# Six instead of four of every sixteen tiles turned on VectorE, with the moves placed elsewhere and the loads divided differently, in an RMSNorm and matmul kernel

## The chip, the cores and the metric

One core of a Trainium2 chip. The metric is the device time of one execution in microseconds; a time in the text is the median of a kernel's runs. The span in a profile, from the first to the last instruction of one profiled execution, is some 2 us shorter (208.1 us in an execution of 210.44 us). Ratios are computed as the mean time of one kernel's fast runs over that of the other's of the same rounds, so they are not quite the ratio of the medians that are quoted.

## The reference

```python
# x: 16 x 1024 x 512 fp32, gamma: 512, weight: 512 x 768, eps 1e-5
rms = np.sqrt(np.mean(x ** 2, axis=-1, keepdims=True) + eps)
x_norm = x / rms * gamma
return np.matmul(x_norm, weight)       # 16 x 1024 x 768 fp32
```

The kernel treats x as 128 tiles of 128 rows. It reads 33.6 MB of x and writes 50.3 MB of results.

## The kernel before

GpSimd casts x to bf16, two bf16 values are treated as one fp32 word, and the tile is turned so that features lie on the partitions. TensorE multiplies the turned tile by the weights (which hold gamma already), and ScalarE (even tiles) or VectorE (odd tiles) scales the product by 1/rms on its way out of PSUM, where the program has TensorE put its products. Three accumulators in PSUM go round. Two tiles make a pair, numbered j; eight pairs make a group of sixteen tiles, which is also the unit of loading.

Twelve tiles of a group (in the first group all sixteen) are turned by TensorE, by transposes put between the matmuls of the pair two earlier, and copied out of PSUM by VectorE. The other four are turned by VectorE alone, in 16 "moves", each of which transposes 32 x 32 blocks (in the page 32 x 256 fp32, 435 ns each).

```python
x_first, x_size = stretches(XG, {0: [2, 2, 4, 8], **{g: [8, 8] for g in (1, 4, 5, 6, 7)}})
# a group that is not named here is one load of 16 tiles, 4 MB
...
def cast_quad(q):                                  # four tiles to be turned on VectorE
    quads[q] = quad_in.tile([P, 4, D], BF16, name="xq")
    nc.gpsimd.tensor_copy(out=quads[q], in_=held(x_tiles, XG, 4 * q, 4))
    ...                                            # puts 16 moves in quad_moves
def move_quad(n):
    for _ in range(min(n, len(quad_moves))):
        dst, src = quad_moves.pop(0)
        nc.vector.transpose(out=dst, in_=src)
...
for j in range(1, NP):
    load_until(...)                                # SyncE issues loads and stores, in this order
    ...                                            # casts of later tiles, GpSimd
    if (2 * j + 2) % XG == 0 and 2 * j + 2 < NT:
        cast_quad((2 * j + 2 + XG - 4) // 4)
    elif 2 * j >= XG:
        move_quad(3)                               # VectorE: moves first ...
    for pair in norm_turns.get(j, []):
        norms_of_group(pair)                       # ScalarE: squares of pair j + 4, from the fp32 load
    ...
    for i, engine in ((2 * j, nc.scalar), (2 * j + 1, nc.vector)):
        a = accumulator()                          # three go round
        matmuls(i, a, range(K), feed)              # feed: transposes of pair j + 2, then VectorE's copy
        finish_tile(i, a, engine)                  # ... then the copy, then the scaling
```

The order on each engine is set by this program. VectorE's scaling stands behind the moves of its pair (in the trace three moves start at 157.97 us, the copy at 159.35, the scaling at 160.08), and ScalarE's scaling behind the squares of a tile four pairs ahead (a square that waited 4.32 us for its load starts at 50.20 us, the scaling behind it at 51.44).

## Time and profile before

| | before |
|---|---|
| time, 3 runs | 210.66 us (210.31 to 210.72) |
| span of the profiled run | 208.1 us |
| TensorE, VectorE, ScalarE busy | 94%, 72%, 69% |
| bytes moved, mean rate | 85.65 MB, 412 GB/s |

The first fence is the page's summary of the chain of work that ended last; the second is from the view of waits, with total us, number and longest.

```profile
PE 71%; DMA 21%; SPq 2%; ACT 1%; POOL 1%; DVE 0%; issue 0%; ACTq 0%; POOLq 0%
```

```profile
POOL xb L94 <- DMA xt<-in_x_dram: 113.0, 16, 18.0
...
PE ops L198 <- ACT ot L178: 2.0, 1, 2.0
```

Once it is running, TensorE waits for another engine for 2.0 us in one place.

### The profile page before, as it was taken

Reading aid. Unit: us, or ns where it says so; the run is one execution under the profiler, and the core shown is the slowest. Engines: PE = TensorE matmul, PEld = TensorE weight load, DVE = VectorE, ACT = ScalarE, POOL = GpSimd, SP = SyncE. Lnnn points to the kernel's source line nnn. Section 1 sums busy time; section 2 is a strip of 40 time slices with the busy share of each in tenths; the row PEclk is TensorE's granted clock in tenths of the full one; section 3 lists DMA queues with packets and bytes.
Section 4 is the critical chain, followed back from the end, with each engine's and each line's share of the span. In section 5 each row is a group of like instructions: output and inputs, shape, how many; then the busy total and the mean of one; then the engine's idle time right before and its main releaser. Section 6 shows DMA issues by size and latency. Waiting matters only on the chain.

```text
span 208.1 us, 3335 instructions
## 1 busy us (share of the span) xinstructions
PE 195.1 (94%) x1238; PEld 129.9 (62%) x1238; DVE 149.6 (72%) x255; ACT 144.5 (69%) x343; POOL 59.9 (29%) x34
## 2 busy tenths in 40 slices
PE   7899999996999999999999999999999999999930
PEld 2466776663666666676667666776667666776610
DVE  0456647997379984999579984999579984999520
ACT  4698897753977877677867877677867877673310
POOL 3237652003900390065200670007500373000000
PEclk9999999999999999999999999999999999999996
DMA  6999999999999999999999999999999999994996
GB/s 252 419 438 441 331 396 435 459 449 390 437 439 438 405 439 409 408 403 431 428 411 436 441 430 430 420 431 439 430 438 408 424 444 435 424 439 203 453 413 267
DMA packets 5490, 85.65 MB, mean 412 GB/s; under 512 B 610, under 2 KB 612, under 8 KB 1380
## 3 DMA queue, kind: packets, MB, share of 16 engines
q1 hardware_dynamic: 5472, 85.46, 97.4%
q8 instruction: 9, 0.15, 0.3%
q14 instruction: 5, 0.04, 0.0%
q10 hardware_dynamic: 4, 0.00, 0.0%
HBM read 35.13 MB, written 50.33 MB: 411 GB/s over the span
## 4 chain that ended last, share of the span: by engine, by line
PE 71%; DMA 21%; SPq 2%; ACT 1%; POOL 1%; DVE 0%; issue 0%; ACTq 0%; POOLq 0%
PE ops L198 63%; DMA xt<-in_x_dram 21%; PE tp L135 8%; SPq L83 1%; POOL xb L94 1%; DVE ot L180 0%; ACT jk L98 0%; SPq L236 0%; ACT ot L178 0%; POOLq L94 0%; ACTq L178 0%; ACTq L98 0%
## 5 line engine op out<-in xcount | busy, mean ns | idle before, releaser
L198 PE MATMUL ops<-w_bf,xT 128*128 128x512 bf16 (+1 forms) x800 | 147.7, 326 | 2.6 <-ACT ot L178 2.0
L198 PEld LDWEIGHTS <-xT 128*128 128x128 bf16 x800 | 78.3, 98 | 48.4 <-issue 3.0
L178 ACT ACTIVATE ot<-ops,rstd 128x768 f32<-128x768 f32 x64 | 57.6, 899 | 45.3 <-PE ops L198 44.6
L98 ACT ACTIVATE jk<-xt 128x512 bf16<-128x512 f32 x128 | 78.8, 619 | 6.2 <-DMA xt<-in_x_dram 6.2
L94 POOL CAST xb<-xt 128x2048 bf16<-128x2048 f32 (+3 forms) x21 | 46.3, 2218 | 113.0 <-DMA xt<-in_x_dram 113.0
L180 DVE TENSOR_SCALAR ot<-ops,rstd 128x768 f32<-128x768 f32 x64 | 64.8, 1013 | 12.5 <-PE ops L198 12.0
L135 PE MATMUL tp<-ident_f,xb 128*128 128x128 f32 x200 | 54.2, 276 | 0.8 <-POOL xb L94 0.7
L142 DVE COPY xT<-tp 128x1024 bf16<-128x1024 bf16 (+1 forms) x53 | 34.5, 654 | 24.8 <-PE tp L135 24.1
L174 DVE STREAM_TRANSPOSE xTq<-xq 32x256 f32<-32x256 f32 x112 | 48.7, 435 | 1.9
L198 PE MATMUL ops<-w_bf,xTq 128*128 128x512 bf16 x224 | 42.8, 326 | 0.0
L135 PEld LDWEIGHTS tp<-ident_f,xb 128*128 128x128 f32 x200 | 28.5, 143 | 4.9 <-POOL xb L94 2.5
L198 PEld LDWEIGHTS <-xTq 128*128 128x128 bf16 x224 | 22.0, 98 | 12.3
L98 ACT ACTIVATION_READ_ACCUMULATOR jk<-xt 128x1 f32 x128 | 24.4, 191 | 0.0
L160 POOL CAST xq<-xt 128x2048 bf16<-128x2048 f32 x7 | 13.3, 1894 | 0.0
L104 DVE RECIPROCAL rstd<-rms 128x8 f32<-128x8 f32 (+3 forms) x20 | 3.9, 193 | 7.7 <-ACT rms L102 7.5
L102 ACT ACTIVATE rms<-ssq,eps_sb 128x8 f32<-128x8 f32 (+3 forms) x20 | 6.0, 299 | 0.6
L254 PE MATMUL ops<-warm 128*128 128x512 bf16 x12 | 5.2, 587 | 1.2 <-DVE eps_sb L247 1.2
L254 PEld LDWEIGHTS <-warm 128*128 128x128 bf16 x12 | 1.4, 128 | 2.9 <-issue 1.7
L178 ACT ACTIVATE w_bf<-w_f,g_sb 128x768 bf16<-128x768 f32 x2 | 1.9, 935 | 1.4 <-DMA w_f<-in_weight_dram 1.1
L267 DVE COPY g_sb<-tp 128x4 f32<-128x4 f32 x1 | 0.2, 161 | 3.2 <-PE tp L265 3.2
L231 ACT ACT_TABLE_LOAD x1 | 1.3, 1283 | 1.3 <-PEq L338 1.3
L180 DVE TENSOR_SCALAR w_bf<-w_f,g_sb 128x512 bf16<-128x512 f32 (+2 forms) x3 | 1.4, 481 | 0.1
(10 smaller groups left out, 1.9 us busy)
## 6 DMA issues: line engine op xcount, KB each, us to landing
out_dram<-ot SPq DMA_DIRECT2D x13, 3072.0 KB, 15.8
xt<-in_x_dram SPq DMA_DIRECT2D x11, 2048.0 KB, 18.5
xt<-in_x_dram SPq DMA_DIRECT2D x2, 4096.0 KB, 20.2
out_dram<-ot SPq DMA_DIRECT2D x5, 1536.0 KB, 9.9
w_f<-in_weight_dram SPq DMA_DIRECT2D x2, 768.0 KB, 5.6
out_dram<-ot SPq DMA_DIRECT2D x2, 768.0 KB, 16.5
xt<-in_x_dram SPq DMA_DIRECT2D x2, 512.0 KB, 5.3
xt<-in_x_dram SPq DMA_DIRECT2D x1, 1024.0 KB, 9.2
```

What stands on the lines that cost most here:

```text
L94: engine.tensor_copy(out=xb_tiles[i // 8][:, i % 8:i % 8 + n, :], in_=held(x_tiles, XG, i, n))
L98: nc.scalar.activation(out=jk, in_=held(x_tiles, XG, i)[:, 0, :], func=AF.Square, accum_out=ssq)
L102: nc.scalar.activation(out=rms[:, :n], in_=ssq[:, :n], func=AF.Sqrt, scale=1.0 / D, bias=eps_sb)
L104: nc.vector.reciprocal(out=rstd[:, :n], in_=rms[:, :n])
L135: nc.tensor.transpose(out=tp_tiles[j][:, t, h, :], in_=words[:, lo:lo + P], identity=ident_f)
L142: nc.vector.tensor_copy(out=dst[:, t:t + n, :], in_=src[:, t:t + n, :])
L160: nc.gpsimd.tensor_copy(out=quads[q], in_=held(x_tiles, XG, 4 * q, 4))
L174: nc.vector.transpose(out=dst, in_=src)
L178: nc.scalar.mul(out=dst, in_=src, mul=r)
L180: nc.vector.tensor_single_scalar(out=dst, in_=src, scalar=r, op=mybir.AluOpType.mult)
L198: nc.tensor.matmul(out=acc[:, lo:hi], lhsT=xT_tiles[i // 2][:, i % 2, k // 2, :, k % 2], rhs=w_bf[:, k, lo:hi], start=(k == 0), stop=(k == ...
L254: nc.tensor.matmul(out=spare[:, :WIDE], lhsT=warm[:, :P], rhs=warm, start=True, stop=True)
```

## The change

Its intent: take two more tiles of each group off TensorE, whose transposes cost it time (by the trace about 0.11 us each); put the moves into the pairs in which TensorE still has transposes, since those last longer (3.04 us against 2.60); and bring tiles 32 to 47 in two loads so that the first half lands earlier.

```diff
-    x_first, x_size = stretches(XG, {0: [2, 2, 4, 8], **{g: [8, 8] for g in (1, 4, 5, 6, 7)}})
+    x_first, x_size = stretches(XG, {0: [2, 2, 4, 8], **{g: [8, 8] for g in (1, 2, 4, 5, 6)}})
 ...
-    B = 32
-    quads, quad_moves = {}, []
+    B, TURNED = 32, 6
+    quad_moves = []
 ...   (cast_to_turn casts six tiles instead of four; still 16 moves, each of half as many elements again)
-            elif j % 8 == 6 and j + 2 < NP:
-                cast(2 * j + 12, nc.gpsimd, 4)
-            if (2 * j + 2) % XG == 0 and 2 * j + 2 < NT:
-                cast_quad((2 * j + 2 + XG - 4) // 4)
-            elif 2 * j >= XG:
-                move_quad(3)
+            elif j % 8 == 5 and j + 3 < NP:
+                cast_to_turn(j // 8 + 1)
+                cast(2 * j + 14, nc.gpsimd, 2)
+            if j > 6:
+                move_quad({3: 4, 4: 0, 5: 0}.get(j % 8, 3))
 ...
-            elif j + 2 < NP and quad_of(j + 2) is None:
+            elif j + 2 < NP and not turned_on_vector(j + 2):
```

The list of groups in eights gains group 2 and loses group 7 (tiles 112 to 127).

More of the change, by code (lines that the diff above doesn't have):

```diff
@@ L148, in transpose_tile, with turned_on_vector, cast_to_turn @@
         evac(i // 2, i % 2, 1)
-    B = 32
-    quads, quad_moves = {}, []
-    def quad_of(j):
-        return j // 2 if (2 * j) % XG >= XG - 4 and 2 * j >= XG else None
-    def cast_quad(q):
-        quads[q] = quad_in.tile([P, 4, D], BF16, name="xq")
-        nc.gpsimd.tensor_copy(out=quads[q], in_=held(x_tiles, XG, 4 * q, 4))
-        turned = quad_out.tile([P, 4, 2, P, 2], BF16, name="xTq")
-        for n in range(2):
-            xT_tiles[2 * q + n] = turned[:, 2 * n:2 * n + 2]
-        words = quads.pop(q).rearrange("p t d -> p (t d)").bitcast(F32).rearrange("p (a w) -> p a w", w=P)
+    B, TURNED = 32, 6
+    quad_moves = []
+    def turned_on_vector(j):
+        return (2 * j) % XG >= XG - TURNED and 2 * j >= XG
+    def cast_to_turn(group):
+        first = (group + 1) * XG - TURNED
+        straight = quad_in.tile([P, TURNED, D], BF16, name="xq")
+        nc.gpsimd.tensor_copy(out=straight, in_=held(x_tiles, XG, first, TURNED))
+        turned = quad_out.tile([P, TURNED, 2, P, 2], BF16, name="xTq")
+        for n in range(TURNED // 2):
+            xT_tiles[first // 2 + n] = turned[:, 2 * n:2 * n + 2]
+        words = straight.rearrange("p t d -> p (t d)").bitcast(F32).rearrange("p (a w) -> p a w", w=P)
         out_words = turned.rearrange("p t h m c -> p (t h m c)").bitcast(F32).rearrange("p (a m) -> p a m", m=P)
```

## The prediction

> **What bounds the kernel now.** I read the page first, then the chain of waits in order of time, then VectorE's and GpSimd's timelines. From the page, the engines' totals, the DMA row and the four groups that the change touches:
> ```profile
> PE 195.1 (94%) x1238; PEld 129.9 (62%) x1238; DVE 149.6 (72%) x255; ACT 144.5 (69%) x343; POOL 59.9 (29%) x34
> ...
> DMA  6999999999999999999999999999999999994996
> ...
> L180 DVE TENSOR_SCALAR ot<-ops,rstd 128x768 f32<-128x768 f32 x64 | 64.8, 1013 | 12.5 <-PE ops L198 12.0
> L135 PE MATMUL tp<-ident_f,xb 128*128 128x128 f32 x200 | 54.2, 276 | 0.8 <-POOL xb L94 0.7
> L142 DVE COPY xT<-tp 128x1024 bf16<-128x1024 bf16 (+1 forms) x53 | 34.5, 654 | 24.8 <-PE tp L135 24.1
> L174 DVE STREAM_TRANSPOSE xTq<-xq 32x256 f32<-32x256 f32 x112 | 48.7, 435 | 1.9
> ```
> TensorE is busy 94%, VectorE has slack on average, and the DMA engines are full until nearly the end. The chain of waits, in order of time:
> ```profile
> 29.96 20.16 DMA xt<-in_x_dram
> 50.12 0.02 issue
> ...
> 51.53 0.80 ACT ot L178
> 52.33 0.04 issue
> 52.37 1.68 PE ops L198 x9
> ```
> Up to 50 us the path is the 4 MB load of tiles 32 to 47 landing; from 52.37 on it is TensorE without a gap. In the chain's later rows eight matmuls without transposes take 1.30 us a tile; four matmuls take 0.65 us and four with a transpose 0.76, so a transpose costs TensorE about 0.11 us, not its 276 ns. A group of 16 tiles repeats every 23.42 us: 16 x 1.30 + 24 x 0.11. Below I count in pairs of tiles: 2.60 us without transposes, 3.04 with.
>
> The stall at 50 us teaches what a late load does. ScalarE squares tile 32 at the start of pair 12, before it scales that pair's first output; while it waits, TensorE runs three tiles (three accumulators) and stops 2.0 us at the fourth. From landing (50.12) to TensorE's restart (52.37) are 2.25 us.
>
> VectorE, in the pairs that now carry moves:
> ```profile
> 157.97 1.33 DVE L174 STREAM_TRANSPOSE xTq<-xq 32x256 f32<-32x256 f32 x3
> 159.35 0.69 DVE L142 COPY xT<-tp 128x1024 bf16<-128x1024 bf16 x1
> 160.08 1.02 DVE L180 TENSOR_SCALAR ot<-ops,rstd 128x768 f32<-128x768 f32 x1
> 161.13 1.33 DVE L174 STREAM_TRANSPOSE xTq<-xq 32x256 f32<-32x256 f32 x3
> ```
> The same place comes round after 3.16 us here (9.37 us for three pairs to 167.34, so 3.12 on average) against TensorE's 3.04: VectorE is already full here and falls back 0.1 us a pair. And GpSimd at the last group:
> ```profile
> 164.82 3.60 POOL L94 CAST xb<-xt 128x4096 bf16<-128x4096 f32 x1 [16.21 <-DMA xt<-in_x_dram]
> 169.71 1.89 POOL L94 CAST xb<-xt 128x2048 bf16<-128x2048 f32 x1 [1.29 <-DMA xt<-in_x_dram]
> 171.55 1.89 POOL L160 CAST xq<-xt 128x2048 bf16<-128x2048 f32 x1
> ```
> Each cast begins as its load lands. The first halves land at 115.6, 139.9 and 164.7 us, some 24.5 us apart: the queue is slower than TensorE's 23.42, which eats its lead. The last first half lands at 164.7, just in time for ScalarE at pair 52 (about 165.7).
>
> [...] the trace holds about 427 GB/s from 95 to 189 us, so I take the queue as full: a load's landing is set by the bytes queued before it, not by when TensorE is ready.
>
> **The change part by part.**
> (1) TensorE loses 28 transposes (seven groups, one more pair each): 28 x 0.11 = 3.1 us, 0.43 a group.
> (2) Tiles 32 to 47 arrive in two loads. The first half, queued where it was, lands about 4.9 us sooner (2.1 MB at 427 GB/s), near 45.2, before ScalarE asks at 45.9. The 2.0 us stall goes.
> (3) The list of groups loaded in eights also loses the last one: tiles 112 to 127 now come in one 4 MB load. It is whole only when the old second half was, about 169.6 us. ScalarE restarts TensorE 2.25 us later, at 171.85, with tile 107, which before began near 169.55. After that tile pair 54 begins at 173.15, not 170.86: 2.3 us late, whatever was won earlier. GpSimd agrees: cast of eight tiles 169.7 to 173.3, needed at the start of pair 54.
> (4) Each of the 112 moves has 384 elements for 256: [...]. VectorE's full pair becomes 3.12 + 3 x 0.133 = 3.52 us against 3.04. Before, moves stood in four pairs with transposes and two without; now in five with and one without, so less is made good in between.
> The consequence: an odd tile's accumulator must be scaled before the tile three later starts. Before, moves begin 1.30 us after their pair starts. If they begin at s, the first pair's scaling ends at s + 3.53 (1.73 moves, 0.05, 0.73 copy, 1.02), the fifth's 4 x 3.52 later, at s + 17.61. The pair that needs that accumulator would start 5 x 3.04 + 2.60 = 17.8 us after the first. With s = 1.30 TensorE is held about 1.15 us per group: more than the 0.43 saved. The period becomes about 24.2 us: five steady groups (2 to 6) give back 3.7 us, more than the roughly 1.2 us still in hand at pair 14 (2.0 + 0.43 less a hold of 1.2 in the first group). So by DVE alone pair 54 starts near 173.4, about where the late load puts it.
> (5) Moves now begin two pairs earlier (pair 54, not 56), and their six-tile cast runs behind the eight-tile one. In the last group it ends at 173.3 + 2.75 = 176.0 (2.75: between 1.89 for four tiles and 3.60 for eight). VectorE, in order, waits for it until 176.0 with the copies and scalings behind it. From there 17.61 + 0.05 puts pair 60 at 193.7; before it started at 189.1. Pairs 60 to 63 and the last stores are unchanged.
> Sum: +2.3 (late load) - 0.43 (last group's transposes) + 2.7 (VectorE held to 176.0, then too slow) = +4.6 us. 210.66 + 4.6 = 215.2 us.
>
> **Rivals.**
> A, the intent: the moves hide and TensorE's 3.1 us and the stall's 2.0 come off: 205.6 us. For it: TensorE is 94% busy, VectorE 72%. Against it: the landing at 169.6 and VectorE's 3.12 in just those pairs.
> B, only the load counts: VectorE's lag stays within the accumulators' slack, and its wait in the last group is absorbed: +2.3 - 0.43, some 212.5 us. For it: no VectorE lag stops TensorE now, and a lag of 0.3 us at pair 52 had 1.2 to spare. Against it: the fifth full pair and the cast's end.
> C, moves grow in full proportion, 0.65 us: VectorE's pair is 3.77 us, over 1 us more is lost in every group, VectorE alone sets the pace, and the total is near 219 us. [...]
> D, TensorE's earlier stores slow the loads: little in it, since loads and stores share one queue in program order and it is already full.
>
> **Range and chances.** The late load leaves little room under 212.5. Above that the size hangs on VectorE's pair: 3.35 instead of 3.52 gives 0.7 us less, C several more, and the landing may shift by 0.5 us. The 2% line lies at 214.9, just below my estimate. I predict 215.2 us, 8 times in 10 between 212.9 and 218.0; faster by over 2% 0.04, within 2% 0.41, slower by over 2% 0.55.
>
> **What would show it right or wrong.** The stall at 50 us should be gone, with ScalarE's wait for tile 32 under 0.5 us. The moves should average about 570 ns. TensorE's period in groups 2 to 6 should be near 24.2 us with gaps released by VectorE's scaling; 23.0 would mean that the lag is absorbed (B). ScalarE should wait for the last load, and GpSimd's eight-tile cast begin near 169.7; a start near 165 would refute step 3. VectorE should show idle time ahead of the moves that GpSimd's cast ends, at the last group above all. If the span is below 205, A holds and my reading of the queue is wrong; if the moves take 650 ns, C.

That a move grows by 0.133 us, on which step 4 rests, was not shown by the kernel before: its 112 moves all have one size. The changed kernel's page shows it, 569 ns for 384 elements against 435 for 256, 0.134 us more.

## The result, and the profile after

The changed kernel takes 214.53 us (213.98 to 214.84, 6 runs) against 210.94 us for the kernel before (210.31 to 211.93, 6 runs): ratio 1.0165, 95% interval 1.0137 to 1.0193. Its profiled span is 212.6 us, 4.5 us more.

The lines of the page that answer to those in the prediction:

```profile
PE 193.7 (91%) x1187; PEld 126.1 (59%) x1210; DVE 159.4 (75%) x248; ACT 144.3 (68%) x343; POOL 59.9 (28%) x34
...
DMA  6999999999999999999999999999999999591897
...
DVE 49%; DMA 18%; PE 14%; issue 7%; POOLq 3%; ACT 3%; POOL 2%; SPq 1%; DVEq 0%
...
L181 DVE TENSOR_SCALAR ot<-ops,rstd 128x768 f32<-128x768 f32 x64 | 64.8, 1014 | 24.0 <-PE ops L199 23.1
...
L175 DVE STREAM_TRANSPOSE xTq<-xq 32x384 f32<-32x384 f32 x112 | 63.8, 569 | 5.2 <-POOL xq L161 3.2
...
L135 PE MATMUL tp<-ident_f,xb 128*128 128x128 f32 x172 | 46.7, 277 | 0.6 <-POOL xb L94 0.3
```

VectorE's busy share rose only from 72% to 75%, yet the chain that ended last runs over VectorE for 49% of the span, where it ran over TensorE for 71% before. A share averaged over the span does not show in which pairs an engine is full. The moves take 569 ns, and 28 transposes are gone.

VectorE in the pairs with moves, from its timeline (start, us, what); it answers to the second VectorE fence of the prediction:

```profile
112.83 1.74 DVE L175 STREAM_TRANSPOSE xTq<-xq 32x384 f32<-32x384 f32 x3
114.59 0.69 DVE L142 COPY xT<-tp 128x1024 bf16<-128x1024 bf16 x1
115.32 1.02 DVE L181 TENSOR_SCALAR ot<-ops,rstd 128x768 f32<-128x768 f32 x1
116.37 1.74 DVE L175 STREAM_TRANSPOSE xTq<-xq 32x384 f32<-32x384 f32 x3
```

Here the place comes round after 3.54 us; over the five pairs from 102.43 to 119.85 us the mean is 3.48. TensorE needs 3.04 for such a pair. After the fifth it has to stop, as its timeline shows in brackets (idle time, and what ended it):

```profile
116.04 3.20 PE L199 MATMUL ops<-w_bf,xT 128*128 128x256 bf16 x19
119.87 2.76 PE L199 MATMUL ops<-w_bf,xT 128*128 128x512 bf16 x15 [0.63 <-DVE ot L181]
```

The nineteen matmuls are the last three of pair 34 and the sixteen of pair 35. The next tile, 72, needs the accumulator of tile 69, which VectorE has just scaled. The last group looks different. GpSimd's timeline and then VectorE's:

```profile
170.15 3.60 POOL L94 CAST xb<-xt 128x4096 bf16<-128x4096 f32 x1 [20.63 <-DMA xt<-in_x_dram]
173.70 2.75 POOL L161 CAST xq<-xt 128x3072 bf16<-128x3072 f32 x1
```

```profile
173.76 1.02 DVE L181 TENSOR_SCALAR ot<-ops,rstd 128x768 f32<-128x768 f32 x1 [2.52 <-PE ops L199]
176.48 1.73 DVE L175 STREAM_TRANSPOSE xTq<-xq 32x384 f32<-32x384 f32 x3 [1.70 <-POOL xq L161]
```

The 4 MB load lands at 170.0 us, GpSimd casts eight tiles, then the six, and VectorE's moves start at 176.48, the moment this ends (176.45). Finally the waits:

```profile
ACT jk L98 <- DMA xt<-in_x_dram: 7.1, 4, 3.2
PE ops L199 <- DVE ot L181: 6.6, 14, 0.7
...
PE ops L199 <- ACT ot L179: 0.8, 1, 0.8
```

Fourteen waits of TensorE for VectorE are new. Some records of matmuls are missing (1187 of 1210), so part of the waits may go unlisted; I therefore take distances between VectorE's scalings of odd tiles, one of each group, for the account:

| stage (pair of the odd tile scaled) | before, us | changed, us | difference |
|---|---|---|---|
| pair 13 reached at | 53.87 | 52.36 | -1.51 |
| 13 to 21 | 23.51 | 23.77 | +0.26 |
| 21 to 29 (moves of tiles 58 to 63) | 23.42 | 25.36 | +1.94 |
| 29 to 37 and 37 to 45, each | 23.42 | 23.78 | +0.36 |
| 45 to 53 (last load awaited) | 23.42 | 24.71 | +1.29 |
| 53 to 61 (last group) | 23.42 | 25.57 | +2.15 |
| pair 61 reached at | 194.48 | 199.33 | +4.85 |

So the changed kernel is ahead after the stall at 50 us, gives back 0.4 us in an undisturbed group, and loses most in three places that have to do with a load that is whole.

### The profile page after: what moved, and what is told of

The parts are those of the page before. It is cut to its first block, busy times and chain, and to the rows that moved or that the text cites.

```text
span 212.6 us, 3246 instructions
## 1 busy us (share of the span) xinstructions
PE 193.7 (91%) x1187; PEld 126.1 (59%) x1210; DVE 159.4 (75%) x248; ACT 144.3 (68%) x343; POOL 59.9 (28%) x34
## 4 chain that ended last, share of the span: by engine, by line
DVE 49%; DMA 18%; PE 14%; issue 7%; POOLq 3%; ACT 3%; POOL 2%; SPq 1%; DVEq 0%
DVE xTq L175 24%; DMA xt<-in_x_dram 18%; DVE ot L181 17%; PE ops L199 13%; DVE xT L142 7%; POOLq L352 3%; ACT jk L98 2%; POOL xq L161 1%; DVE rstd L104 1%; POOL xb L94 1%; SPq L83 1%; PE tp L135 1%; SPq L237 0%; ACT ot L179 0%; SPq L196 0%
## 5 line engine op out<-in xcount | busy, mean ns | idle before, releaser
L199 PE MATMUL ops<-w_bf,xT 128*128 128x512 bf16 (+1 forms) x673 | 127.4, 324 | 7.1 <-DVE ot L181 6.0
L199 PEld LDWEIGHTS <-xT 128*128 128x128 bf16 x688 | 67.3, 98 | 46.4 <-issue 7.1
L94 POOL CAST xb<-xt 128x1024 bf16<-128x1024 f32 (+3 forms) x21 | 40.4, 1934 | 108.3 <-DMA xt<-in_x_dram 89.5
L175 DVE STREAM_TRANSPOSE xTq<-xq 32x384 f32<-32x384 f32 x112 | 63.8, 569 | 5.2 <-POOL xq L161 3.2
L199 PE MATMUL ops<-w_bf,xTq 128*128 128x256 bf16 (+1 forms) x328 | 60.8, 324 | 1.8 <-ACT ot L179 0.8
L135 PE MATMUL tp<-ident_f,xb 128*128 128x128 f32 x172 | 46.7, 277 | 0.6 <-POOL xb L94 0.3
L199 PEld LDWEIGHTS <-xTq 128*128 128x128 bf16 x336 | 32.9, 98 | 21.3 <-issue 1.8
L142 DVE COPY xT<-tp 128x1024 bf16<-128x1024 bf16 (+1 forms) x46 | 29.1, 633 | 6.9 <-PE tp L135 6.4
L135 PEld LDWEIGHTS tp<-ident_f,xb 128*128 128x128 f32 x172 | 24.5, 143 | 6.5 <-POOL xb L94 2.3
L161 POOL CAST xq<-xt 128x3072 bf16<-128x3072 f32 x7 | 19.2, 2747 | 8.7 <-DMA xt<-in_x_dram 5.8
```

The source lines that it names most:

```text
L94: engine.tensor_copy(out=xb_tiles[i // 8][:, i % 8:i % 8 + n, :], in_=held(x_tiles, XG, i, n))
L135: nc.tensor.transpose(out=tp_tiles[j][:, t, h, :], in_=words[:, lo:lo + P], identity=ident_f)
L142: nc.vector.tensor_copy(out=dst[:, t:t + n, :], in_=src[:, t:t + n, :])
L161: nc.gpsimd.tensor_copy(out=straight, in_=held(x_tiles, XG, first, TURNED))
L199: nc.tensor.matmul(out=acc[:, lo:hi], lhsT=xT_tiles[i // 2][:, i % 2, k // 2, :, k % 2], rhs=w_bf[:, k, lo:hi], start=(k == 0), stop=(k == ...
```

## The experiments

Two theories of the slowdown were open besides the intended gain: the whole last load, and VectorE's overfull pairs. With the two kernels, the first four runs cross three lists of loads (that of the kernel before, that of the changed one, and both groups in eights) with the two ways of turning. The kernel before took 210.77 us in the rounds of these four (7 runs).

**1. The kernel before, group 2 in eights.**

```diff
-g in (1, 4, 5, 6, 7)
+g in (1, 2, 4, 5, 6, 7)
```

> The kernel before with one change: tiles 32 to 47 in two loads of eight (the last group stays in eights). Theory (the queue is full and in order, VectorE does not hold TensorE): the 2.0 us stall at 50 us goes and nothing takes its place, because the last first half still lands near 164.7 us and ScalarE then asks at about 163.0 us, which three tiles of accumulators cover. Expect 208.6 us (ratio 0.990), no wait of TensorE for ScalarE at 50 us. Rival (the stall is only moved: TensorE runs into the loads later): 210.5 us, with a new TensorE wait near 165 us.

Measured: 210.47 us (209.86 to 210.90), ratio 0.997 (0.9924 to 1.0016). The theory's time is a miss, though its mechanism is there: the stall is gone, TensorE waits for nobody at 165 us, and VectorE starts the last scaling at 197.56 us instead of 199.68. The rival's new wait near 165 us is not there either. The 2.1 us are lost after the last scaling. The view of windows shows it. Its columns are the stretch and its length in us, the busy time of TensorE, its weight loads, VectorE, ScalarE and GpSimd (with the number of instructions), the granted clock, the share of the 16 DMA engines' time, and GB/s. First the kernel before, then this one:

```profile
188.00:189.00 1.00, 1.00 (x9) 0.66 (x7) 0.94 (x4) 0.66 (x1) 0.00 (x0) 1.00 0.63 270
189.00:190.00 1.00, 1.00 (x8) 0.61 (x7) 0.97 (x2) 0.00 (x0) 0.00 (x0) 1.00 0.29 123
190.00:191.00 1.00, 1.00 (x8) 0.61 (x7) 0.97 (x2) 0.42 (x1) 0.00 (x0) 1.00 0.12 49
```

```profile
188.00:189.00 1.00, 1.00 (x8) 0.61 (x7) 0.97 (x2) 0.54 (x1) 0.00 (x0) 1.00 0.35 147
189.00:190.00 1.00, 1.00 (x8) 0.60 (x7) 0.96 (x3) 0.36 (x1) 0.00 (x0) 1.00 0.98 418
...
204.00:205.00 1.00, 0.00 (x0) 0.00 (x0) 0.00 (x0) 0.00 (x0) 0.00 (x0) 0.50 0.27 111
205.00:206.00 1.00, 0.00 (x0) 0.00 (x0) 0.00 (x0) 0.00 (x0) 0.00 (x0) 0.50 0.12 49
206.00:207.00 1.00, 0.00 (x0) 0.00 (x0) 0.00 (x0) 0.00 (x0) 0.00 (x0) 0.50 0.03 12
```

Before, the engines are partly idle from 188 to 191 us (shares 0.63, 0.29 and 0.12), as the store of tiles 112 to 119 is issued only at 190.80 us. Here that store comes 2.1 us sooner, at 188.68; at the end the share falls to 0.27, 0.12 and 0.03, but something is moved until 207. In the kernel before the same stretches from 204 to 206 us still move 430 and 479 GB/s. The last store lands at 207.34 us, against 207.21 before. So the DMA transfers, not TensorE, end last, and they end at 49 and 12 GB/s. By the shares, 0.12 would be two of the 16 engines and 0.03 half of one; that a few engines lag is an estimate of mine from these shares, since the trace does not tell packets by engine. The two runs 8 and 9 test whether the transfers set the end.

**2. The kernel before, with the changed kernel's list of loads.**

```diff
-g in (1, 4, 5, 6, 7)
+g in (1, 2, 4, 5, 6)
```

> The kernel before with the changed kernel's whole list of loads: tiles 32 to 47 in eights, tiles 112 to 127 in one 4 MB load; four tiles turned as before. Theory (the whole last load costs by itself): ScalarE waits for it until about 169.7 us and TensorE stops some 4 us near 168 us, so 2.3 us more than before: 212.9 us (ratio 1.011). Rival (the whole load is hidden by VectorE or by the lead, only the moves cost): as with eights throughout, 208.6 us.

Measured: 213.74 us (213.65 to 213.90), ratio 1.0129 (1.0078 to 1.0179). The theory holds: the whole load costs by itself, without any change to the moves. ScalarE's timeline and TensorE's:

```profile
169.23 0.63 ACT L98 ACTIVATE jk<-xt 128x512 bf16<-128x512 f32 x1 [6.30 <-DMA xt<-in_x_dram]
```

```profile
171.40 2.22 PE L198 MATMUL ops<-w_bf,xT 128*128 128x512 bf16 x8 [3.99 <-ACT ot L178]
```

From the start of the squares to TensorE's restart are 2.2 us, as at 50 us in the kernel before. The time is 0.8 us above what was expected, and one cause is in view: after the stop of 4.0 us the granted clock is 0.67 from 171.4 to 173, 0.50 until 175 and 0.82 until 176, and the eight matmuls take 2.22 us. After the stop of 2.0 us in the kernel before the clock stayed at 1.00 (52.4 to 56 us), and the same eight took 1.46. How long a stop has to be for the clock to fall is not shown.

**3. The changed kernel, last group in eights.** (Diff of the same list, to (1, 2, 4, 5, 6, 7).)

> The changed kernel with the last group in eights again. Theory: the first half lands near 165 us, the six-tile cast ends near 172.9 us instead of 176.4, VectorE does not wait for it in the last group, and the last group takes 23.8 us like the steady ones; TensorE's own wait for ScalarE at 172 us goes as well. Expect 2.5 to 3 us less than the changed kernel, 211.8 us (ratio to before 1.005). Rival (the load is not on the path, VectorE alone sets the pace): 214.3 us.

Measured: 211.73 us (211.27 to 212.43), ratio 1.0035 (0.9986 to 1.0084), 2.8 us less than the changed kernel, as the theory said. The last two stages take 23.77 and 23.78 us; VectorE no longer waits for the cast in the last group. The group 21 to 29, whose load is still whole, takes 25.24.

**4. The changed kernel, with the kernel before's list of loads.** (To (1, 4, 5, 6, 7).)

> The changed kernel with the kernel before's list of loads: tiles 32 to 47 in one load, the last group in eights; only the moves differ from the kernel before. Theory: the stall at 50 us is back (TensorE restarts near 52.4 us, some 1.5 us later than in the changed kernel), the last group is as with eights: 1.3 us above that one, 213.1 us (ratio 1.012), so six tiles alone cost 2.4 us. Rival (TensorE's 28 transposes are won, 3.1 us): 207.6 us.

Measured: 213.70 us (212.88 to 214.11), ratio 1.012 (1.0072 to 1.0169). With the old loads six tiles cost, and the rival is out. The size is 0.6 us above expectation. The profiled run was the fastest of the four, so what the slower ones met is not shown. But the cost is not of the moves alone: the stage 13 to 21 takes 25.57 us, the other five 23.77 to 23.78, because VectorE waits there for the six-tile cast behind the whole load of tiles 32 to 47:

```profile
55.75 1.73 DVE L175 STREAM_TRANSPOSE xTq<-xq 32x384 f32<-32x384 f32 x3 [1.70 <-POOL xq L161]
```

Tiles 48 to 63, one load here too, cost nothing (21 to 29 takes 23.78 us), since pair 21 comes 2.5 us later than in the changed kernel (78.59 us instead of 76.13). In these runs a whole load cost only where the program reached it before its cast was done.

**5. The changed kernel, all groups in eights.** (To (1, 2, 3, 4, 5, 6, 7).) The kernel before took 210.84 us in the rounds of runs 5 to 8.

> The changed kernel with every group loaded in eights, tiles 48 to 63 too. Theory (a whole load is late for the moves, which now come two pairs earlier): the group of tiles 48 to 63 takes 23.8 us like the others instead of 25.2, so the last scaling is at 200.9 us and not 202.3, and 1.4 us come off the run with the last group alone in eights: 210.3 us (ratio 0.998). All groups then take 23.8 us: what is left is VectorE's hold of 0.8 us against 0.44 saved. Rival (the queue shifts the wait elsewhere): 211.7 us, no gain.

Measured: 211.25 us (210.95 to 211.81), ratio 1.0021 (0.9989 to 1.0053). The stage 21 to 29 fell to 23.78 us as expected, so its excess in the changed kernel was due to its whole load, met as early as it is there (run 4). The time fell less, to between what the theory (210.3) and the rival (211.7) had: the profiled run starts its last scaling at 201.41 us instead of the expected 200.9, the last group taking 24.14 us, and the difference to run 3 (0.5 us between medians) is within the runs' scatter.

**6. All groups in eights, and the moves spread.** In place of 3, 3, 3, 3, 3, 1 moves from the seventh pair of a group on:

```diff
-                move_quad({3: 4, 4: 0, 5: 0}.get(j % 8, 3))
+                first = {7: 3, 8: 3, 9: 3, 10: 2, 11: 3, 12: 2}
+                steady = {6: 3, 7: 3, 0: 2, 1: 2, 2: 2, 3: 3, 4: 1}
+                move_quad(first.get(j, 0) if j < 14 else steady.get(j % 8, 0))
```

> All groups in eights, and six tiles turned as in the changed kernel, but the 16 moves of a group are spread 3, 3, 2, 2, 2, 3, 1 over seven pairs (two of them without TensorE transposes) instead of 3, 3, 3, 3, 3, 1. Theory (an overfull VectorE pair, 3.48 us against 3.04, holds TensorE): with two moves the pair is 2.9 us and the hold at the end of a group goes; groups 2 to 5 take 23.0 to 23.2 us, unless a landing stops them. TensorE then meets the last group's loads and the full queue, so the time falls little: 210.2 us, last scaling near 199.2. Rival (the hold comes from the moves' total of 9.1 us a group, not from their place): groups stay at 23.8 us.

Measured: 210.29 us (210.05 to 211.08), ratio 0.9979 (0.9946 to 1.0012). From the view of waits:

```profile
PE ops L199 <- DVE xTq L175: 3.1, 4, 1.0
...
PE ops L199 <- DVE ot L181: 1.0, 3, 0.3
```

In run 5, TensorE waited 4.7 us for VectorE's scalings, eight times. Here three short ones are left, at 152, 155 and 180 us, and a new wait has come: for a move that now ends too close to its use, 1.05 us at 50 us and 0.7 at 143, 168 and 192 us. The stages 13 to 37 take 23.01 us each: VectorE does the same work, and TensorE's saving of 0.4 us per group comes through. So the place of the moves, not their total, made the hold. The later stages take 24.0 to 24.9 us, as TensorE, now earlier, meets the landings: ScalarE waits 1.5 us at 165.38, and VectorE 1.7 to 1.8 us for the casts of the last two groups.

**7. The changed kernel, moves of the last group one pair later.**

```diff
+            if j > 53:
+                move_quad({55: 3, 56: 3, 57: 3, 58: 3, 59: 4}.get(j, 0))
-            if j > 6:
+            elif j > 6:
```

> The changed kernel, with one edit in the last group alone: its moves begin one pair later (3, 3, 3, 3, 4 from pair 55 on), so that VectorE no longer waits for GpSimd's six-tile cast; the whole 4 MB load stays. Theory (that wait is on the path): VectorE's wait of 1.7 us ahead of the moves goes; its backlog holds TensorE 1.2 us by itself instead of 2.4 us; 1.2 to 1.8 us come off: 213.0 us (ratio 1.010). Rival (TensorE's wait for ScalarE and the late load alone set the last group): 214.5 us.

Measured: 213.99 us (213.77 to 214.16), ratio 1.0147 (1.0118 to 1.0177). The wait is gone, and the last scaling begins at 202.87 us, 1.66 us sooner: the wait for the cast was on TensorE's path, with the expected size. But the time fell by only 0.5 us. The store of tiles 112 to 119 left at 194.88 us, only 0.7 us sooner than in the changed kernel (four moves of pair 59 stand ahead of its last scaling), and the three last stores then landed 3.7 us apart, at the queue's pace (1.57 MB each, so some 425 GB/s): 203.58, 207.28, 210.95.

**8. Run 1 with less to store, and 9, its control.** Both leave out the store of tiles 96 to 103 (3.1 MB), so the result is wrong. No load stands behind it in the queue.

```diff
-        if i == first + n - 1:
+        if i == first + n - 1 and first != 96:
```

> The kernel before with tiles 32 to 47 in eights, and the store of tiles 96 to 103 left out (3.1 MB; those rows of the result are wrong on purpose). No load stands behind that store. Theory (with the stall gone TensorE ends 2.1 us earlier, but the DMA queue, full to the end, hands back the same total): with less to store the 2.1 us show: 208.5 us (ratio 0.990). Rival (something else at the end holds it, or the earlier end of TensorE was the profiled run's alone): as with the store, 210.3 us.

> The kernel before, all else untouched, with the store of tiles 96 to 103 left out (wrong on purpose). It is the control to the same omission with tiles 32 to 47 in eights, which took 207.3 us. Theory (here TensorE, not the queue, sets the end, and the queue stood at most 0.4 us above it): 210.2 us, 0.2 to 0.5 us less than the kernel before, the last scaling still at 199.7 us. Rival (leaving 3.1 MB out saves 3 us anywhere, stall or no stall): 207.5 us.

Measured: with group 2 in eights 207.32 us (207.27 to 207.44), ratio 0.9831 (0.9803 to 0.9859); the kernel before with the same omission 209.77 us (209.54 to 211.31), ratio 0.9970 (0.9943 to 0.9997). The same 3.1 MB are worth 0.3% where TensorE ends late and, beside run 10, 1.5% where it ends early. That settles run 1: its 2.1 us of TensorE are real, and the DMA engines' total keeps them from being seen. Both times lie below what was expected, by 1.2 us (run 8) and 0.4 (run 9). The profiled spans fell by 2.6 and 0.7 us; the rest of run 8's surplus is not explained, and the kernel before scattered from 210.37 to 212.05 us in its rounds. Of run 9's 0.7 us, 0.45 come of its stall, which happened to be 1.7 us instead of 2.0, so the kernel before stood about 0.3 us from the limit.

The traces say more exactly what sets the end. Take the moment at which SyncE issues the store of tiles 112 to 119, the third from last; 6.3 MB then remain to be stored. In nine of the thirteen profiles (the changed kernel and runs 2 to 9) the span ends 16.9 to 17.1 us after it, and at most one DMA packet of older stores is still in flight at that moment; in the kernel before, with two in flight, it is 17.3 us. In runs 1, 10 and 11, with 6 to 9 in flight, it is 19.2 to 19.7 us. The three last stores land 3.6 to 3.7 us apart in every run that shows their landings, so from this issue on the queue sets the pace. Run 7 tells it apart from TensorE's end: there the last scaling comes 8.0 us after the issue instead of 8.9 in the changed kernel, and the span still ends 17.0 after it. For the changed kernel this gives the account: its store is issued at 195.59 us instead of 190.80, 4.8 us later, less the 0.3, which is the 4.5 us of the span.

**10. Run 1 again, with five rounds,** where the kernel before took 210.61 us (11 runs, also for run 9 and 11).

> The kernel before with tiles 32 to 47 in eights, once more, with more rounds and beside the others of this call. Theory (TensorE ends 2.1 us sooner, the queue gives at most 0.4 us of it): 210.2 to 210.6 us, ratio 0.996 to 0.999. Rival (2.0 us come through in most runs): 208.6 us.

Measured: 210.48 us (209.89 to 210.83), ratio 0.9982 (0.9963 to 1.0001). As the theory said.

**11. Fewer short transfers.** If the queue sets the end, joining its short transfers might help, even though TensorE then starts later; that is a guess, which this run tests.

```diff
-    x_first, x_size = stretches(XG, {0: [2, 2, 4, 8], **{g: [8, 8] for g in (1, 4, 5, 6, 7)}})
-    o_first, o_size = stretches(OG, {0: [2, 2, 4], 1: [4, 4], last: [4, 4]})
+    x_first, x_size = stretches(XG, {0: [4, 4, 8], **{g: [8, 8] for g in (1, 2, 4, 5, 6, 7)}})
+    o_first, o_size = stretches(OG, {0: [4, 4], last: [4, 4]})
```

> Tiles 32 to 47 in eights, and the short transfers at the start joined: first loads of 4, 4, 8 tiles instead of 2, 2, 4, 8; first stores of 4, 4 and 8 tiles instead of 2, 2, 4, 4, 4. TensorE starts about 1.2 us later, which the 2.1 us won by the eights cover. Theory (the queue sets the end, and its slow stretch from 21 to 26 us, 350 GB/s for 430, comes of the short packets): the queue's total falls by about 1 us, 209.5 us (ratio 0.993). Rival (the slow stretch comes of the turn from reading to writing, or of something else): 210.4 us, as with the eights alone; worse than that if TensorE's later start reaches the end.

Measured: 209.80 us (209.38 to 209.98), ratio 0.9952 (0.9934 to 0.9970). It is the fastest of the correct kernels, ahead of both, though by half a per cent. The last store lands 0.76 us sooner than in run 10. The slow stretch from 21 to 26 us goes from 349 GB/s in run 10 to 379, not to 430; but run 9, whose start is that of the kernel before, shows 386 in the same slice of its page, where the kernel before shows 331. So that short packets make the slow stretch is not shown, and where the half per cent comes from stays open.

## Why the prediction was right or wrong

The time, 214.53 us, lies in the range and 0.7 us below the estimate. The change counted as most likely, slower by over 2%, did not come: the ratio is 1.0165. In the profiled runs the span grew by 4.5 us against the 4.6 predicted; the medians differ by only 3.6, since the kernel before took 211.2 to 211.9 us in the three runs added beside the changed one. My estimate stood 0.3 us above the 2% line, so the chances could hardly have leaned further to one side than they did, and the line fell the other way.

Step 1 (transposes): right, 200 became 172, and run 6 shows the saving alone, 23.42 to 23.01 us a group.

Step 2 (stall at 50 us): right, the half load landed at 44.67 us and TensorE waited no more for ScalarE there. What was missed is that this would have gained nothing by itself (runs 1, 8, 9, 10).

Step 3 (last load whole): right. It landed at 170.0 instead of 169.6 us, and TensorE restarted at 172.26 instead of 171.85. Runs 2 and 3 show it as a cause: 2.8 us from taking it back.

Step 4 (VectorE's pair): the mechanism was right, and run 6 shows it by moving the moves. Two terms of the sum were too large. The pair measured 3.48 us, not 3.52, and the moves began 1.15 us after their pair, not 1.30. Four times 0.04 and 0.15 make 0.31. The sum itself was also rounded up: its own terms, 1.30 + 17.61 - 17.80, make 1.11 and not 1.15. 1.11 less 0.31 is 0.80, and that is the hold measured (23.78 less 22.98 without it); the group took 23.8 us instead of 24.2.

Step 5 (moves behind the late cast): right in the last group, where the cast ended at 176.45 instead of 176.0 us, and pair 60 began at 193.9 instead of 193.7. But the same step was not applied to tiles 48 to 63, which were one load in both kernels. There, too, the moves now come two pairs earlier and waited 1.49 us for the cast; the group cost 1.6 us more than its neighbours, which run 5 takes away. In run 4, where TensorE comes later, the same load costs nothing: what the half load won at 50 us (1.5 us by pair 13) was handed back here at once. This omission and the oversized hold nearly cancelled by pair 53: five groups were to give back 3.7 us, and from pair 13 to 53 they gave back 4.2, of which 0.9 belong to the late load. The close total is thus partly luck.

Of the rivals, A had no way to come true with these stores. Even with TensorE 2.1 us earlier the time stays near 210.5 us, as the end of the DMA queue is then the bound (the last store lands at 207.34 us in run 1, at 207.21 in the kernel before). I used the full queue as an argument about landings and did not ask what it means for the end. B is answered by run 7: VectorE's wait is not absorbed for TensorE. C is out: 569 ns a move, where full proportion makes 650. With the 435 ns at 256 elements that is 1.05 ns for each further element and, by an estimate from these two sizes, some 167 ns that do not grow. D shows no sign: in run 1 the stores leave some 2 us sooner, and the last load lands at 169.8 us, in the kernel before near 169.6.

What stays open: whether single DMA engines lag at the end of run 1, and why, since the trace does not tell packets by engine; what slows the queue near 21 to 26 us in every kernel; and why joined transfers help.

## What to carry to other kernels

Ask of an engine with slack on average whether it has slack in the very pairs into which work is moved; here, where VectorE's scaling stands behind its moves, a surplus of 0.44 us a pair (3.48 against 3.04), five times in a row, used up the three accumulators and held TensorE 0.8 us a group. When work is moved earlier, check which load it now stands behind, in every group and not only the one edited. And before counting a gain on the busiest engine, work out what the other full resource allows: here TensorE could end 2.1 us sooner, and the DMA queue gave nearly all of it back (210.48 us in run 10, 210.61 in the kernel before). Where stores end a kernel, date it by the issue of the last ones and by what is still queued ahead of them, not by the last instruction that computes: here the span ended 16.9 to 17.1 us after that issue with at most one older packet in flight, and 19.2 to 19.7 us after it with 6 to 9.
